# One layer of a hybrid decoder on one core: a written order for the matmuls of the up projection, other buffers for its stored products, and row loads of the down projection tied to the fifth step

## The chip, the core and the metric

The kernel runs on one core of a Trainium2 chip. The metric is device microseconds from the start to the end of one execution; the median of several executions is compared. The core's engines are TensorE (PE, with its weight loads listed as PEld), VectorE (DVE), ScalarE (ACT), GpSimd (POOL) and SyncE (SP). Each works through its own instructions in order; semaphores tie them together. DMA transfers are started here by SP, ACT and POOL.

## The reference

One layer over 1024 positions of width 1024 in float32. The change lies in the last sublayer, a gated feed-forward network with a short causal convolution over positions:

```python
def conv_ffn(h, w_up, dw_w, dw_b, w_down):
    u = causal_dwconv(h @ w_up, dw_w, dw_b)        # FFN_CONV = 3 taps
    gate, val = jnp.split(u, 2, axis=-1)           # 2 x FFN_DIM, FFN_DIM = 2816
    return (jax.nn.silu(gate) * val) @ w_down

    mix = (sigmoid(gate_a) * y_a + sigmoid(gate_b) * y_b) @ w_o[l]
    h = layer_norm(DN_ALPHA * h + mix, ln1_g[l], ln1_b[l])
    h = layer_norm(DN_ALPHA * h + conv_ffn(h, ...), ln2_g[l], ln2_b[l])
```

Before it stand a convolution branch and a state-space branch, which the change doesn't touch.

## The kernel before

**Numbers in two parts.** Every large product is made of float32 operands split into a rounded part and a rest (`split_pair`, L737: ACT casts, DVE subtracts), and `mm3` (L163) issues three matmuls for one product of 128 x 128 by 128 x 512. A product of four contraction tiles (`product`, L725) has 12 matmuls.

**Up projection.** It is done by a scheme with seven products in place of eight: the tokens are cut in halves (early, late), the contraction in halves, and a pair of channel tiles (one gate, one value) makes the 2 x 2 of the weights. `ffn_blocks` (L744) makes the blocks of the activations: b11 and b21 are the two halves of the early tokens, b22 and t1 to t4 are blocks and sums for the late ones. There are NF = 22 pairs. A pair is:

- `up_weights` (L834): two loads (`ra`, `rb`, 512 KB each, in rings `st` and `raw` of three buffers), four additions on DVE, and splits into ue (first weights as they are; from pair 8 on), w24, w10 and w3. ue, w24 and w10 share a ring of three buffers, tag `w` of the pool wsp; w3 has a ring of two.
- `up_rest` (L857): the products. ps is a PSUM bank of the ring `acc` (four), pz one of the ring `sm` (four). b11 goes into ps and is copied to s by ACT; b21 goes into another bank and is added to s for the early tokens of the gate; t2 is added onto ps and copied to s again; t3 goes to pz; t1 onto ps, copied to the value's late tokens; t4 onto pz; b22 onto ps, copied to the gate's late tokens. Then the three taps of the convolution, SiLU and gating (L889 to L916) on ACT and DVE, and the stores of the results, or of sums of two pairs' results, to DRAM (`b11_scr`, `b2_scr`, `t32_scr`, `t41_scr`) from POOL and SP. The gate and the value tile of a pair live in two of three buffers u, in turn, so a pair's gate takes the buffer of the value tile of the pair before.

**The stored products.** For the first LEAD = 8 pairs, `up_first` (L815) computes b11 and b11 + b21 earlier, while the block sums are still being made: two products into one bank, a copy by ACT after each (L831) into a tile `first`, and a store to `first_scr` (L832) from ACT's queue. `first` has a ring of two in a pool of its own, "firsts", on the right side of the memory (L1134). The pair then loads both halves from DRAM into u with one DMA (L874), and ACT copies the late half into ps (L878), where t2 is added onto it.

**The memory.** Pools are stacked from the left or from the right. "trans", the pool of `ffn_blocks`, is on the left and closed before "up" is opened (L1128 to L1130), so both start at the same place; a tile of "up" waits for those tiles of "trans" whose bytes it takes. A pool lays out its tags in the order in which they are first used. In "trans": two gains of 4 KB a partition, three row buffers of 4 KB (tiles r0 to r7; the second buffer is used last by r5, the third by r7), then 16 KB of raw blocks and the temporaries of the sums. In "up": three u of 4224 bytes, then the others.

**Down projection.** `down` (L930) has seven products p = 0 to 6 of eleven steps; a step loads weights and activations (`load`, L974), splits them into w and issues 12 matmuls, three into each of four banks. Its results are combined with the 1024 rows of the residual stream, which `load_rows` (L950) brings from `h1_scr` with four DMAs of 256 KB from POOL, in the code after the fifth step (k = 4) of p = 0, 1, 2 and 4, into one tile `rows`; nothing but the space of that tile holds them back.

**The order.** The program's order on each engine is made by a planner: among the instructions whose inputs it reckons to be there, it takes the one with the lowest number; `tc.high_priority(offset=n)` lowers the number by n. Buffers of a ring are handed out in the order of the code. A block `tc.manual_schedule(engines={PE})` keeps PE's instructions in it in the order of the code.

The products of a pair, before:

```python
ps, pz = bank(1), bank(0)
...
product(ps, lambda i: w24[:, i, :HALF], bl["t2"], False)
A.copy(s, ps)
product(pz, lambda i: w3[:, i], bl["t3"], True)
product(ps, lambda i: w10[:, i, :HALF], bl["t1"], False)
A.copy(uv[:, late], ps)
V.tensor_tensor(out=uv[:, late], in0=pz, in1=uv[:, late], op=ALU.subtract)
product(pz, lambda i: w10[:, i, HALF:], bl["t4"], False)
V.tensor_tensor(out=uv[:, early], in0=pz, in1=s, op=ALU.subtract)
product(ps, lambda i: w24[:, i, HALF:], bl["b22"], False)
A.copy(ug[:, late], ps)
```

Of the kernel before, what the change touches and what calls it, by code (L numbers as in the profile page):

```python
# [16 lines left out]
P = 128  # L17
D = 1024
# [38 lines left out]
def kernel(  # L57
# [17 lines left out]
    def pool(name, bufs=1, **kw):  # L75
        return tc.tile_pool(name=name, bufs=bufs, reuse_waits="tile", **kw)
# [11 lines left out]
    def bank(which):  # L88
        n_ps[0] += 1
        pl, tag = (pacc, "acc") if which else (psm, "sm")  # L90
        return pl.tile([P, 512], F32, tag=tag, name=f"{tag}{n_ps[0]}")
# [633 lines left out]
    def product(ps, w, xs, first):  # L725

        for k in range(4):
            mm3(
                ps,
                lambda i: w(i)[:, k * P : (k + 1) * P],  # L730
                lambda i: xs(i)[:, k, :],
                first and k == 0,
                k == 3,
                not first,
            )
# [76 lines left out]
            "t4": lambda i: b2[0][:, i, 4:8, :],  # L812
        }

    def up_first(upp, fp, bl, j):  # L815

        if j < LEAD - 1:
            t = weights(wup[2 * j], f"ue{j}")
            w = [t[:, i, :] for i in range(2)]
        else:  # L820
            with tc.high_priority(offset=4000):
                st = wst.tile([P, D], F32, tag="st", name=f"st_ue{j}")
                SY.dma_start(st, wup[2 * j])
                w = [upp.tile([P, D], F32R, tag="o", bufs=3, name=f"ue{i}_{j}") for i in range(2)]
                A.copy(w[0], st)
                V.tensor_tensor(out=w[1], in0=st, in1=w[0].bitcast(F32), op=ALU.subtract)
        ps = bank(1)
        for q, block in enumerate(("b11", "b21")):
            product(ps, lambda i: w[i][:, q * HALF : (q + 1) * HALF], bl[block], q == 0)
            f = fp.tile([P, HALF], F32, tag="first", bufs=2, name=f"first{q}_{j}")  # L830
            A.copy(f, ps)  # L831
            A.dma_start(first_scr[j][1 - q], f)  # L832

    def up_weights(upp, j):  # L834


        with tc.high_priority(offset=2000):
            r1 = wst.tile([P, D], F32, tag="st", name=f"ra{j}")
            SY.dma_start(r1, wup[2 * j])
            if j:  # L840
                r2 = upp.tile([P, D], F32, tag="raw", bufs=3, name=f"rb{j}")
            else:
                r2 = wst.tile([P, D], F32, tag="st", name=f"rb{j}")
            SY.dma_start(r2, wup[2 * j + 1])
            a11, a12, a21, a22 = r1[:, :HALF], r1[:, HALF:], r2[:, :HALF], r2[:, HALF:]
            ue = None if j < LEAD else split_pair(wsp, r1, f"ue{j}")
            s3 = upp.tile([P, HALF], F32, tag="s3", name=f"s3_{j}")
            V.tensor_tensor(out=s3, in0=a11, in1=a21, op=ALU.add)
            V.tensor_tensor(out=a21, in0=a21, in1=a22, op=ALU.add)
            V.tensor_tensor(out=a11, in0=a21, in1=a11, op=ALU.add)  # L850
            V.tensor_tensor(out=a12, in0=a12, in1=a11, op=ALU.add)
            w24 = split_pair(wsp, r1, f"s24_{j}")
            w10 = split_pair(wsp, r2, f"s10_{j}")
            w3 = split_pair(upp, s3, f"s3_{j}", HALF, 2)
        return ue, w24, w10, w3

    def up_rest(upp, us, bl, j, before, ws):  # L857

        ue, w24, w10, w3 = ws or up_weights(upp, j)
        ug, uv = us[2 * j % 3], us[(2 * j + 1) % 3]
        s = upp.tile([P, HALF], F32, tag="s", bufs=2, name=f"s{j}")
        early, late = slice(2, 2 + HALF), slice(2 + HALF, 2 + T)
        ps, pz = bank(1), bank(0)
        if ue:
            product(ps, lambda i: ue[:, i, :HALF], bl["b11"], True)
            A.copy(s, ps)
            py = bank(1)
            product(py, lambda i: ue[:, i, HALF:], bl["b21"], True)  # L870
            V.tensor_tensor(out=ug[:, early], in0=s, in1=py, op=ALU.add)
        else:
            with tc.high_priority(offset=2500):
                SY.dma_start(  # L874
                    ug[:, 2 : 2 + T].rearrange("p (q n) -> p q n", q=2),
                    first_scr[j].rearrange("q p n -> p q n"),
                )
            A.copy(ps, ug[:, late])  # L878
        product(ps, lambda i: w24[:, i, :HALF], bl["t2"], False)
        A.copy(s, ps)  # L880
        product(pz, lambda i: w3[:, i], bl["t3"], True)
        product(ps, lambda i: w10[:, i, :HALF], bl["t1"], False)
        A.copy(uv[:, late], ps)
        V.tensor_tensor(out=uv[:, late], in0=pz, in1=uv[:, late], op=ALU.subtract)
        product(pz, lambda i: w10[:, i, HALF:], bl["t4"], False)
        V.tensor_tensor(out=uv[:, early], in0=pz, in1=s, op=ALU.subtract)
        product(ps, lambda i: w24[:, i, HALF:], bl["b22"], False)
        A.copy(ug[:, late], ps)
        os = []  # L889
        j = j // 2 + j % 2 * NK  # L890
        for jj, u in ((j, ug), (NF + j, uv)):
            o = upp.tile([P, T], F32, tag="o", bufs=3, name=f"fo{jj}")
            wc = PC_FW + 3 * jj
            A.activation(  # L894
                out=o, in_=u[:, 2 : 2 + T], func=AF.Identity, scale=pc[:, wc + 2 : wc + 3]
            )
            for k in range(2):
                V.scalar_tensor_tensor(  # L898
                    out=o,
                    in0=u[:, k : k + T],  # L900
                    scalar=pc[:, wc + k : wc + k + 1],
                    in1=o,
                    op0=ALU.mult,
                    op1=ALU.add,
                )
            os.append(o)
        og, ov = os
        A.activation(out=og, in_=og, func=AF.Silu, bias=pc[:, PC_FB + j : PC_FB + j + 1])
        V.scalar_tensor_tensor(
            out=ov,  # L910
            in0=ov,
            scalar=pc[:, PC_FB + NF + j : PC_FB + NF + j + 1],
            in1=og,
            op0=ALU.add,
            op1=ALU.mult,
        )  # L916
        early, late = slice(0, HALF), slice(HALF, T)
        if j < NK:
            G.dma_start(b11_scr[j], ov[:, early])
            return ov  # L920
        SY.dma_start(b2_scr[j - NK], ov)
        a, b, t = before, ov, og
        V.tensor_tensor(out=t[:, early], in0=a[:, late], in1=b[:, late], op=ALU.subtract)
        V.tensor_tensor(out=a[:, late], in0=a[:, early], in1=a[:, late], op=ALU.subtract)
        V.tensor_tensor(out=t[:, late], in0=t[:, early], in1=a[:, early], op=ALU.subtract)
        V.tensor_tensor(out=a[:, early], in0=b[:, early], in1=t[:, late], op=ALU.add)
        G.dma_start(t32_scr[j - NK], t)
        G.dma_start(t41_scr[j - NK], a)

    def down(upp, dp):  # L930
# [16 lines left out]
        E, L = slice(0, HALF), slice(HALF, D)  # L947
        gb = []

        def load_rows(p):  # L950
            t0, cs = {0: (0, E), 1: (0, L), 2: (4, L), 4: (4, E)}[p]
            for t in range(t0, t0 + 4):
                G.dma_start(rs[t][:, cs], h1_scr[t * P : (t + 1) * P, cs])
            if p == 2:
                for n, start in (("g", RW_2G), ("b", RW_2B)):
                    r = upp.tile([P, D], F32, tag="o", bufs=3, name=f"ln2_{n}")
                    G.dma_start(r, prow[start : start + D].partition_broadcast(P))
                    gb.append(r)
# [132 lines left out]
        for p, (banks, first, then) in enumerate(products):  # L1091
            end = NK - LAST if p == 6 else NK
            for k in range(end):
                w = load(p, k)
                for t in range(4):
                    block(banks[t], w, t, first, k)
                if k == 4 and p in (0, 1, 2, 4):
                    load_rows(p)
            ws = {k: load(p, k) for k in range(end, NK)}
            for t in range(4):  # L1100
                for k in ws:
                    block(banks[t], ws[k], t, first, k)
                then(t)
# [27 lines left out]
    us = [upp.tile([P, T + 32], F32, name=f"u{i}") for i in range(3)]  # L1131
    for u in us:
        G.memset(u[:, :2], 0.0)
    with pool("firsts", side="right") as fp:  # L1134
        for j in range(LEAD):
            if j == LEAD - 1:
                ws = up_weights(upp, 0)
            up_first(upp, fp, bl, j)
    before = None
    for j in range(NF):  # L1140
        before, ws = up_rest(upp, us, bl, j, before, ws), None
    ffn_stack.close()
    dp = ctx.enter_context(pool("down", side="right"))
    down(upp, dp)
# [99 lines left out]
```

## Time and profile before

| what | us |
| --- | --- |
| median of 3 executions | 2024.91 (2024.34 to 2026.39) |
| profiled execution | 2030.47 |
| its span, first to last instruction | 2028.8 |
| first matmul of `up_first` in it | 1350.3 |
| last copy of a stored product | 1407.4 |
| first and last row load (L953) issued | 1805.4, 1820.0 |

The profile is of one execution. Its rows give, for each engine, when an instruction started and how long it ran, and in brackets how long the engine had stood idle before and which instruction ended that. Busy time is the time in which an engine ran something; matmuls overlap one another, so their starts say more than their lengths. A row of a window gives its length, then for each engine the busy time and the number of instructions, then the clock that PE was granted (1.00 is full), the busy share of the 16 DMA engines and the GB/s they moved. Some per cent of the matmul records can be missing.

### The profile page before, as it was taken

What the parts mean: (1) busy time and instruction counts of PE and PEld (TensorE: products, weight loads), DVE (VectorE), ACT (ScalarE), POOL (GpSimd) and SP (SyncE); (2) the same over time, 40 slices, a digit from 0 to 9 for tenths busy, and PEclk for the clock granted to TensorE, in tenths of its full rate; (3) what the DMA queues carried; (4) which work ended last, traced back from release to release, by engine and by line L of the source; (5) the groups of instructions that cost most, each with busy time, mean ns of one, the idle gap of its engine ahead of it and who ended that gap; (6) DMA issues with size and microseconds to landing.
All of it is one profiled execution on the core that took longest, in us unless ns stands there. A gap on an engine that the chain in (4) does not pass through costs nothing.

```text
span 2028.8 us, 24542 instructions
## 1 busy us (share of the span) xinstructions
PE 1975.8 (97%) x9164; PEld 1622.4 (80%) x9164; DVE 1695.8 (84%) x2261; ACT 1017.4 (50%) x1480; POOL 175.5 (9%) x140
## 2 busy tenths in 40 slices
PE   7999999999999999999999999999999999999998
PEld 6888888888788888888888888887777777777886
DVE  7599999989766869999998976596897777788768
ACT  4465654556453356665454645364554534443432
POOL 2010101001400000110100130010000000030000
PEclk9999999999999999999999999999999999999999
DMA  6222233333546522222323354565342222367563
GB/s 219 94 64 93 79 103 104 99 104 101 175 131 220 194 94 73 91 81 77 126 89 104 109 167 139 186 234 202 135 172 83 99 107 102 101 252 252 176 225 109
DMA packets 96903, 272.20 MB, mean 134 GB/s; under 512 B 11088, under 2 KB 11088, under 8 KB 96784
## 3 DMA queue, kind: packets, MB, share of 16 engines
q1 hardware_dynamic: 88864, 246.78, 36.8%
q0 software_dynamic: 5616, 19.66, 2.5%
q10 hardware_dynamic: 2304, 4.20, 0.6%
q8 instruction: 72, 1.18, 0.2%
q14 instruction: 47, 0.39, 0.1%
HBM read 221.05 MB, written 49.55 MB: 133 GB/s over the span
## 4 chain that ended last, share of the span: by engine, by line
PE 72%; DVE 19%; DMA 4%; issue 3%; ACT 2%; SPq 0%; DVEq 0%; ACTq 0%
PE acc L166 19%; PE acc L167 19%; PE acc L168 19%; DVE c L420 6%; PE sm L168 3%; PE sm L166 3%; PE sm L167 3%; PE sm L534 2%; PE acc L357 1%; DVE xbc L375 1%; DVE fo L898 1%; DMA dr<-b_scr 1%; PE sm L515 1%; PE sm L192 1%; PE sm L523 1%
## 5 line engine op out<-in xcount | busy, mean ns | idle before, releaser
L420 DVE SCALAR_TENSOR_TENSOR c<-v,pc,c 128x512 f32<-128x512 f32 x480 | 374.9, 804 | 6.3 <-ACT c L409 4.9
L478 POOL TENSOR_TENSOR au<-seg_mv,head_of 128x1024 fp32r<-128x1024 f32 x32 | 76.4, 2388 | 959.1 <-PE sm L487 728.8
L166 PE MATMUL acc<-hT,w_c 128*128 128x512 f32 x352 | 141.0, 401 | 0.0
L167 PE MATMUL acc<-hT,w_c 128*128 128x512 f32 x352 | 140.6, 399 | 0.0
L168 PE MATMUL acc<-hT,w_c 128*128 128x512 f32 x352 | 138.4, 393 | 0.0
L898 DVE SCALAR_TENSOR_TENSOR fo<-u,pc,fo 128x1024 f32<-128x1024 f32 x88 | 111.4, 1279 | 7.5 <-ACT fo L894 7.4
L375 DVE SCALAR_TENSOR_TENSOR xbc<-u,pc,xbc 128x512 f32<-128x512 f32 x144 | 109.9, 775 | 0.7 <-ACT xbc L373 0.5
L166 PE MATMUL acc<-h1s,w_s 128*128 128x512 f32 x264 | 103.6, 396 | 6.3 <-ACT s L880 3.7
L167 PE MATMUL acc<-h1s,w_s 128*128 128x512 f32 x264 | 102.9, 390 | 0.0
L168 PE MATMUL acc<-h1s,w_s 128*128 128x512 f32 x264 | 102.8, 391 | 0.0
L167 PE MATMUL acc<-w_z,hT 128*128 128x512 f32 x256 | 100.8, 394 | 0.0
L166 PE MATMUL acc<-w_z,hT 128*128 128x512 f32 x256 | 100.8, 401 | 0.0
L168 PE MATMUL acc<-w_z,hT 128*128 128x512 f32 x256 | 100.7, 396 | 0.0
L1032 ACT CAST w_dn<-dr 128x1024 fp32r<-128x1024 f32 (+1 forms) x73 | 60.9, 842 | 75.8 <-DVE dr L962 37.8
L154 ACT CAST w_c<-st_c 128x1024 fp32r<-128x1024 f32 x50 | 52.5, 1051 | 88.9 <-PE acc L168 68.2
L1033 DVE TENSOR_TENSOR w_dn<-dr,w_dn 128x1024 fp32r<-128x1024 f32 (+1 forms) x73 | 69.8, 963 | 15.3 <-ACT w_dn L1032 15.1
L167 PEld LDWEIGHTS acc<-hT,w_c 128*128 128x128 f32 x352 | 66.1, 188 | 16.9 <-issue 3.9
L168 PEld LDWEIGHTS acc<-hT,w_c 128*128 128x128 f32 x352 | 66.1, 188 | 16.2 <-issue 2.6
L166 PEld LDWEIGHTS acc<-hT,w_c 128*128 128x128 f32 x352 | 66.1, 188 | 15.9 <-issue 2.6
L166 PE MATMUL acc<-h1b,w_ue 128*128 128x512 f32 x168 | 67.3, 400 | 11.1 <-ACT w_ue L740 8.4
L155 DVE TENSOR_TENSOR w_c<-st_c,w_c 128x1024 fp32r<-128x1024 f32 x47 | 60.5, 1288 | 20.2 <-ACT w_c L154 20.2
L740 ACT CAST w_s<-rb 128x1024 fp32r<-128x1024 f32 x22 | 23.0, 1048 | 98.4 <-PE sm L168 63.8
(353 smaller groups left out, 5755.4 us busy)
## 6 DMA issues: line engine op xcount, KB each, us to landing
st_c<-wcol SPq DMA_DIRECT2D x50, 512.0 KB, 3.5
st_z<-wz SPq DMA_DIRECT2D x32, 512.0 KB, 3.5
st_wo<-wo SPq DMA_DIRECT2D x24, 512.0 KB, 4.0
ra<-wup SPq DMA_DIRECT2D x22, 512.0 KB, 3.6
rb<-wup SPq DMA_DIRECT2D x22, 512.0 KB, 3.4
t_scr<-fo POOLq DMA_DIRECT2D x22, 512.0 KB, 3.8
dr<-t_scr SPq DMA_DIRECT2D x44, 256.0 KB, 3.5
dr<-wdown SPq DMA_DIRECT2D x38, 256.0 KB, 3.9
```

The lines of the kernel that those rows point to most:

```text
L154: A.copy(w[:, 0, :], st)
L155: (eng or V).tensor_tensor(out=w[:, 1, :], in0=st, in1=w[:, 0, :].bitcast(F32), op=ALU.subtract)
L166: TE.matmul(ps, wa(0), xa(0), start=start, stop=False, skip_group_check=more)
L167: TE.matmul(ps, wa(0), xa(1), start=False, stop=False, skip_group_check=more)
L168: TE.matmul(ps, wa(1), xa(0), start=False, stop=stop, skip_group_check=more)
L375: V.scalar_tensor_tensor(out=o, in0=u[:, k : k + HALF], scalar=pc[:, wc + k : wc + k + 1], in1=o, op0=ALU.mult, op1=ALU.add,)
L420: V.scalar_tensor_tensor(out=accs[i], in0=v[:, k : k + HALF], scalar=pc[:, wc + k : wc + k + 1], in1=accs[i], op0=ALU.mult, op1=ALU.add,)
L478: G.tensor_tensor(out=au, in0=seg_mv[:, c, :].unsqueeze(1).to_broadcast([P, 8, P]), in1=head_of[:, g, :].unsqueeze(2).to_broadcast([P, 8, P]),
L534: TE.matmul(py[:, hs], m[:, h, :], xs[:, hs], start=True, stop=True)
L898: V.scalar_tensor_tensor(out=o, in0=u[:, k : k + T], scalar=pc[:, wc + k : wc + k + 1], in1=o, op0=ALU.mult, op1=ALU.add,)
L1032: A.copy(w[:, 0, cs], src)
L1033: V.tensor_tensor(out=w[:, 1, cs], in0=src, in1=w[:, 0, cs].bitcast(F32), op=ALU.subtract)
```

## The change

The stored products take buffers of the ring `s` in the pool "up", which now has three; the pool "firsts" is gone. The order of the two halves in `first_scr` is turned. A pair of the first eight loads the b11 half into its tile s (not into u), copies it into ps from there, and loads the other half into the early tokens of u with a second DMA. The pair's function becomes a generator in three parts, and the caller lays the parts of two pairs over each other: b11 of pair j + 1 (t2 for the first eight); then b22 and t4 of pair j; then b21, t2, t3, t1 of pair j + 1 (t3, t1 for the first eight). b22 now stands before t4. PE keeps that order. Some copies and subtractions get a priority of 300. In the down projection, before the four row loads POOL copies four numbers of the fifth step's w into the first column of the four row blocks, so the loads wait for that w.

```diff
-    def up_first(upp, fp, bl, j):
+    def up_first(upp, bl, j):
-            f = fp.tile([P, HALF], F32, tag="first", bufs=2, name=f"first{q}_{j}")
+            f = upp.tile([P, HALF], F32, tag="s", bufs=3, name=f"first{q}_{j}")
             A.copy(f, ps)
-            A.dma_start(first_scr[j][1 - q], f)
+            A.dma_start(first_scr[j][q], f)
...
-    def up_rest(upp, us, bl, j, before, ws):
+    def up_pair(upp, us, bl, j, kept, ws):
-        s = upp.tile([P, HALF], F32, tag="s", bufs=2, name=f"s{j}")
+        s = upp.tile([P, HALF], F32, tag="s", bufs=3, name=f"s{j}")
+        def t2():
+            product(ps, lambda i: w24[:, i, :HALF], bl["t2"], False)
+            with tc.high_priority(offset=300):
+                A.copy(s, ps)
         if ue:
             product(ps, lambda i: ue[:, i, :HALF], bl["b11"], True)
-            A.copy(s, ps)
+            with tc.high_priority(offset=300):
+                A.copy(s, ps)
+        else:
+            with tc.high_priority(offset=2500):
+                SY.dma_start(s, first_scr[j][0])
+            with tc.high_priority(offset=300):
+                A.copy(ps, s)
+            SY.dma_start(ug[:, early], first_scr[j][1])
+            t2()
+        yield
+        if ue:
             py = bank(1)
             product(py, lambda i: ue[:, i, HALF:], bl["b21"], True)
-            V.tensor_tensor(out=ug[:, early], in0=s, in1=py, op=ALU.add)
-        else:
-            with tc.high_priority(offset=2500):
-                SY.dma_start(
-                    ug[:, 2 : 2 + T].rearrange("p (q n) -> p q n", q=2),
-                    first_scr[j].rearrange("q p n -> p q n"),
-                )
-            A.copy(ps, ug[:, late])
-        product(ps, lambda i: w24[:, i, :HALF], bl["t2"], False)
-        A.copy(s, ps)
+            with tc.high_priority(offset=300):
+                V.tensor_tensor(out=ug[:, early], in0=s, in1=py, op=ALU.add)
+            t2()
         product(pz, lambda i: w3[:, i], bl["t3"], True)
         product(ps, lambda i: w10[:, i, :HALF], bl["t1"], False)
-        A.copy(uv[:, late], ps)
-        V.tensor_tensor(out=uv[:, late], in0=pz, in1=uv[:, late], op=ALU.subtract)
+        with tc.high_priority(offset=300):
+            A.copy(uv[:, late], ps)
+            V.tensor_tensor(out=uv[:, late], in0=pz, in1=uv[:, late], op=ALU.subtract)
+        yield
+        product(ps, lambda i: w24[:, i, HALF:], bl["b22"], False)
+        A.copy(ug[:, late], ps)
         product(pz, lambda i: w10[:, i, HALF:], bl["t4"], False)
         V.tensor_tensor(out=uv[:, early], in0=pz, in1=s, op=ALU.subtract)
-        product(ps, lambda i: w24[:, i, HALF:], bl["b22"], False)
-        A.copy(ug[:, late], ps)
...
-        def load_rows(p):
+        def load_rows(p, w):
             t0, cs = {0: (0, E), 1: (0, L), 2: (4, L), 4: (4, E)}[p]
+            G.tensor_copy(
+                rows.rearrange("p (t n) -> p t n", n=D)[:, t0 : t0 + 4, cs.start : cs.start + 1],
+                w[:, 0, :4].bitcast(F32).unsqueeze(2),
+            )
...
-    with pool("firsts", side="right") as fp:
-        for j in range(LEAD):
-            if j == LEAD - 1:
-                ws = up_weights(upp, 0)
-            up_first(upp, fp, bl, j)
-    before = None
-    for j in range(NF):
-        before, ws = up_rest(upp, us, bl, j, before, ws), None
+    for j in range(LEAD):
+        if j == LEAD - 1:
+            ws = up_weights(upp, 0)
+        up_first(upp, bl, j)
+    kept = []
+    with tc.manual_schedule(engines={mybir.EngineType.PE}):
+        pairs = [up_pair(upp, us, bl, 0, kept, ws)]
+        next(pairs[0])
+        next(pairs[0])
+        for j in range(1, NF + 1):
+            if j < NF:
+                pairs.append(up_pair(upp, us, bl, j, kept, None))
+                next(pairs[j])
+            next(pairs[j - 1], None)
+            if j < NF:
+                next(pairs[j])
```

More of the change, by code (lines that the diff above doesn't have):

```diff
@@ L919, in up_rest @@
             G.dma_start(b11_scr[j], ov[:, early])
-            return ov
+            kept.append(ov)
+            return
         SY.dma_start(b2_scr[j - NK], ov)
-        a, b, t = before, ov, og
+        a, b, t = kept.pop(), ov, og
         V.tensor_tensor(out=t[:, early], in0=a[:, late], in1=b[:, late], op=ALU.subtract)
@@ L1097, in down @@
                 if k == 4 and p in (0, 1, 2, 4):
-                    load_rows(p)
+                    load_rows(p, w)
             ws = {k: load(p, k) for k in range(end, NK)}
```

## The prediction

> **What bounds the kernel now.** I read first the page's busy times and the chain that ended last, then a table of windows over the end of the kernel, then who TensorE (PE) waits for.
>
> ```profile
> span 2028.8 us, 24542 instructions
> PE 1975.8 (97%) x9164; PEld 1622.4 (80%) x9164; DVE 1695.8 (84%) x2261; ACT 1017.4 (50%) x1480; POOL 175.5 (9%) x140
> PE 72%; DVE 19%; DMA 4%; issue 3%; ACT 2%; SPq 0%; DVEq 0%; ACTq 0%
> ```
>
> PE is busy for 97% of the span, and 72% of the chain is PE. The change leaves the number of matmuls as it is, so it can only gain where PE stands still or runs at a low clock, and lose by adding such places. The windows show where these are in the stages that the diff touches.
>
> ```profile
> core 0: us, PE busy (x) PEld busy (x) DVE busy (x) ACT busy (x) POOL busy (x), PEclk, DMA share, GB/s
> 1388.70:1391.50 2.80, 0.07 (x2) 0.04 (x1) 2.27 (x4) 1.17 (x2) 0.00 (x0) 0.85 1.03 417
> 1391.50:1397.40 5.90, 5.90 (x14) 4.64 (x15) 3.44 (x4) 3.45 (x5) 0.00 (x0) 0.50 0.82 303
> 1408.00:1514.00 106.00, 98.65 (x420) 77.51 (x419) 85.85 (x101) 51.84 (x66) 3.95 (x7) 1.00 0.40 139
> 1514.00:1762.00 248.00, 239.59 (x1042) 194.59 (x1041) 193.11 (x222) 112.34 (x137) 10.65 (x20) 1.00 0.29 102
> 1762.00:1796.00 34.00, 33.06 (x143) 26.42 (x142) 28.21 (x29) 16.58 (x20) 6.23 (x7) 1.00 0.47 162
> 1796.00:1806.00 10.00, 9.80 (x43) 7.79 (x42) 8.79 (x10) 6.27 (x9) 2.81 (x4) 1.00 0.26 81
> 1806.00:1824.00 18.00, 17.95 (x79) 14.54 (x79) 14.90 (x18) 9.31 (x13) 8.08 (x15) 1.00 1.02 383
> 1824.00:1836.00 12.00, 8.62 (x27) 6.52 (x26) 7.50 (x13) 4.88 (x9) 1.03 (x2) 0.72 0.81 269
> ```
>
> The yardstick is the step between matmuls of a dense stretch:
>
> ```profile
> 1620.33 0.39 PE L166 MATMUL acc<-h1b,w_ue 128*128 128x512 f32 x1
> 1623.05 0.39 PE L168 MATMUL acc<-h1b,w_ue 128*128 128x512 f32 x1
> ```
>
> Between these two starts lie 12 steps, 2.72 us: 0.227 us a matmul, 2.72 us a product of 12. A window's loss is its length less its count times 0.227.
>
> - First eight pairs (1408 to 1514): 106 - 420 x 0.227 = **10.7 us** lost.
> - Later pairs (1514 to 1762): 248 - 1042 x 0.227 = **11.5 us**.
> - Last pairs (1762 to 1806): 44 - 186 x 0.227 = **1.8 us**.
> - First product of the down stage (1806 to 1836): 30 - 106 x 0.227 = **5.9 us**.
> - Before the pairs: 2.8 us empty, then 14 matmuls in 5.9 us at clock 0.50 where 26 fit, 2.7 us more: **5.5 us**.
>
> Who ended PE's waits from 1200 us on:
>
> ```profile
> PE acc L166 <- ACT w_ue L740: 8.4, 6, 1.4
> PE acc L166 <- ACT s L880: 3.7, 5, 0.9
> PE acc L166 <- ACT w_dn L1032: 3.4, 1, 3.4
> PE acc L166 <- ACT first L831: 2.7, 1, 2.7
> PE acc L166 <- ACT u L883: 2.7, 3, 1.7
> ACT acc L878 <- DMA u<-first_scr: 20.1, 5, 4.5
> ```
>
> A row gives the total in us, the number of waits and the longest. The last row is from 1408 to 1514: the stored product is loaded into u itself, so the load waits until the convolution two tiles earlier has read u, and ACT can fill the bank only then.
>
> **Part by part: later pairs.** Once in 40 us PE reaches the b11 product before its weights are split.
>
> ```profile
> 1637.44 0.39 PE L168 MATMUL acc<-h1s,w_s 128*128 128x512 f32 x1
> 1639.23 0.50 PE L166 MATMUL acc<-h1b,w_ue 128*128 128x512 f32 x1 [1.40 <-ACT w_ue L740]
> 1637.19 1.05 ACT L740 CAST w_s<-rb 128x1024 fp32r<-128x1024 f32 x1 [9.72 <-PE sm L168]
> 1638.14 1.04 ACT L740 CAST w_ue<-ra 128x1024 fp32r<-128x1024 f32 x1
> ```
>
> The step across it is 1.79 us instead of 0.23, with a slow restart of 0.1: 1.67 us, six times, 10.0 of the 11.5. In the written order (b11 of j+1; b22, t4 of j; b21, t2, t3, t1 of j+1) the buffer of ue is free after b21, and t2, t3, t1 (8.2 us) cover the cast and the split. w24 is free after b22 with two products behind it (5.4 us), w10 after t4 with three. Copies of s and u have one product (2.72 us) of cover. What may be late next is the subtraction that frees s: DVE is 78% busy here (193.11 of 248). I take **9 us** gained (bounds 4 and 11.5).
>
> **First eight pairs.** Loading into s removes the chain convolution, DMA, ACT. The load of u's early half still waits for it, but only the next convolution needs that. It becomes two DMAs for one: eight more issues on SP, off the path. DVE is late next: 85.85 us for 420 matmuls is 12.3 us per 60, against 13.6 us of PE, 90%. I take **8 of 10.7** (bounds 0 and 10.7).
>
> **Last pairs.** t1 and b22 of pair 21 follow each other with no pair between, so a copy's wait of about 0.7 us (3.7/5) stays: **1 of 1.8**.
>
> **Down.** All sixteen row loads went out when their tile became free, and share the DMA engines with the loads that PE needs.
>
> ```profile
> 1805.38 3.78 POOL L953 DMA_DIRECT2D rows<-h_scr  x7 [1.70 <-PE sm L168]
> 1819.98 0.55 POOL L953 DMA_DIRECT2D rows<-h_scr  x1 [0.56 <-DMA rows<-h_scr]
> 1812.67 15.16 DMA dr<-b_scr
> dr<-b_scr SPq DMA_DIRECT2D x18, 256.0 KB, 6.9
> L993 POOL COPY c<-dr x5: 614/1517/1646, 1782.0 to 1796.7; 128x512 f32<-128x512 f32 x5
> 1866.00:1896.00 30.00, 30.00 (x134) 24.84 (x133) 28.98 (x42) 12.09 (x16) 0.00 (x0) 1.00 0.60 186
> ```
>
> From 1806 to 1824 the DMA engines are full (share 1.02, 383 GB/s); one load takes 15.16 us instead of the median 6.9, PE waits 3.4 us for its cast, and clock 0.72 follows. With 12 of 16 loads (3 MB, 8 us at 383 GB/s) sent later, that load lands before it is needed. The small copy that ties them is on POOL, busy 9%: four elements a partition, between nothing and the 1.5 us of 512 elements, four times, hidden. It holds a weight buffer until POOL runs; if POOL stands before a store's wait, PE waits too. The rows now fall into products two, three and five, where the DMA share is 0.60 and PE is dense: 0 to 3 us. I take **5 of 5.9** gained (bounds 1 and 5.9).
>
> The Trainium skill, "DMA: Bandwidth & Descriptors", section "Issuing engines are not separate DMA queues", says that transfers issued by different engines share the same 16 DMA engines; the full share at 1806 agrees, and by that rule 3 MB later is work moved, not removed.
>
> **The stored products.** Here I expect a loss. Before, `first` has a pool of its own on the right, free while the block sums are made. After, it takes s buffers of the pool `up`, which lies where the pool `trans` lay. By the tile sizes in the code, u takes 12.4 KB from the common start and the three s buffers 12.4 to 18.4; `trans` has 8 KB of gains, then three row buffers of 4 KB (8 to 20), the second last used by r5, the third by r7. So the first s buffer is free after r5, the two others only after r7 is transposed and stored. That `up` waits for `trans` can be seen: the memsets of u, with no other input, run at 1379.84 on an idle POOL.
>
> ```profile
> 1379.84 0.18 POOL L1133 MEMSET u<- 128x2 f32 x3
> 1370.96 0.33 SPq L779 DMA_DIRECT2D h_scr<-r  x1
> h_scr<-r SPq DMA_DIRECT2D x2, 512.0 KB, 3.4
> L831 ACT COPY first<-acc x16: 573/586/595, 1353.4 to 1407.4; 128x512 f32<-128x512 f32 x16
> DMA to landing us min/median/max: 2.0/3.7/7.0
> 1388.01 0.50 PE L166 MATMUL sm<-h1b,w_s 128*128 128x512 f32 x1
> 1401.73 0.39 PE L166 MATMUL acc<-h1s,w_s 128*128 128x512 f32 x1
> ```
>
> (The fourth row groups the 16 copies of `first`, with first and last start; the landing row is of the transfers through `first_scr`.) r7's store starts at 1370.96 and lands 3.4 us later, 1374.4. Until then PE has four banks and one buffer: five products (b11 of j 0 to 3, b21 of j 0). The second copy ends at 1375.0; eleven products take 29.9 us (1404.9), and after the idle stretch the clock costs 2.7 us as at 1391 (1407.6). Then PE has nothing: s of pair 0 stands sixteen tiles behind `first` in one ring and its buffer comes in the order of the code, t2 of pair 0 is first in the written order, and it needs copy 0.6, load 3.7, copy 0.6: 1412.5, and 2.7 for the clock again: 1415.2. Before, the firsts ended at 1407.2 with t3 and t2 of pair 0 (rows at 1388.01 and 1401.73) done, 5.4 us: as if at 1401.8. The loss is **13 us**, with the 5.5 us of the old gap in it. Bounds: -4 (buffers free as before, and the old gap gone) and 31 (below). Behind the waiting copy on ACT stand casts of block sums and of the next ue, which the order has at their own times, so I charge nothing for them; behind the load of s on SP stand weight loads for pairs 1 and 2, which PE reaches over 13 us later; behind t2 on PE stands everything.
>
> The Trainium skill, "TensorE: Matmul & The Clock Gate", section "HAM oscillation — how this bites in real kernels", says to avoid idle gaps above about 3.4 us. Here a gap of 2.8 us already brought the clock to 0.50. By the page the waits reckoned above, over 4 us each, cost the clock too: the same sum.
>
> **Sum.** -9 - 8 - 1 - 5 + 13 = -10 us, on a profiled execution of 2030.47 us (span 2028.8), which is 0.27% above the median of 2024.91. I take the same 10 us from the median: **2015 us**.
>
> **Rivals.**
> A. The buffers are not held (the planner lets the firsts go on in the one free buffer, or r7 is early). Then only the wait for s of pair 0 stays, 4.9 + 2.7 less the old 5.5: 2 us lost instead of 13, 2004 us. For it: a copy and its store take 0.6 + 4 us, less than two products. Against it: the memsets at 1379.84, and the ring's order.
> B. Slower: all three buffers are held until the last tile of `trans` is read, about 1386 (first cast into `up`, row below). PE then stops after three products (three weight buffers), and thirteen follow: 1386 + 0.6 + 35.4 + 2.7 + 4.9 + 2.7 = 1432, 31 us lost: +8, 2033 us. It decides as soon as the release is 10 us later than 1374.4, after which the 23 us of gains are used up. For it: tiles of `up` start only at 1379 to 1386. Against it: these lie under other tiles than s does.
>
> ```profile
> 1385.88 1.05 ACT L825 CAST ue<-st_ue 128x1024 fp32r<-128x1024 f32 x1
> ```
>
> C. The order does not do what it is written for: DVE, 90% needed in the first eight pairs and in order, becomes the bound, and PE, also in order, cannot go round it. Those pairs keep 106 us per 420 matmuls: 8 us less gain, 2023 us. For it: 85.85 us of DVE. Against it: its waits there are for PE and ACT.
>
> **How the numbers follow.** Forecast 0.48, A 0.19, B 0.15, C 0.18. Low end: A with the upper gains, 2002; high end: near B, 2031. 0.2% (4 us) is about what a measurement of this kernel can tell from no change. Faster by more: 0.43 of the forecast and A, 0.62. Within: 0.05 of the forecast, 0.15 of C, 0.02 of B, 0.22. Slower: 0.13 of B, 0.03 of C, 0.16.
>
> **What the profile after would show.** If I am right: the first copies of L831 come at about 1353, 1374 and 1375; PE is empty for 8 us before 1375 and for 4 to 5 us before the first t2, with low clock behind both; no wait for w_ue in the later pairs; fewer waits in the first eight, at a DVE busy by 90%; row loads in four groups of four, and no wait for w_dn near 1828. A second copy at 1360 would make A right, at 1386 B. A start loss of 5 or 25 us, or pairs at 15 us, would make the forecast wrong.

## The result, and the profile after

The changed kernel takes 2034.92 us (median of 6 executions, 2032.61 to 2038.66); the kernel before, measured beside it, 2026.31 us (6 executions, 2024.34 to 2028.77). The ratio is 1.0044, 95% interval 1.0031 to 1.0056: 9 us slower. The forecast was 10 us faster, and the time lies above the top of the range. The profiled execution of the changed kernel took 2038.66 us.

Its page, the span, the busy times and the chain that ended last:

```profile
span 2036.9 us, 24591 instructions
PE 1975.9 (97%) x9164; PEld 1627.6 (80%) x9164; DVE 1695.1 (83%) x2261; ACT 1022.6 (50%) x1480; POOL 177.7 (9%) x144
PE 74%; DVE 19%; issue 3%; DMA 2%; ACT 1%; SPq 0%; POOL 0%; DVEq 0%; ACTq 0%; POOLq 0%
```

Of this page only the span says that anything went wrong: busy shares are averages over the whole kernel, and 8 us in 2037 are not seen in them. The table of windows says where to look (columns as in the prediction: length; busy time and count of PE, PEld, DVE, ACT, POOL; clock; DMA share; GB/s):

```profile
1362.00:1374.00 12.00, 4.12 (x18) 3.36 (x18) 12.00 (x18) 2.19 (x5) 2.31 (x1) 0.73 0.21 73
1374.00:1386.00 12.00, 2.14 (x10) 1.57 (x8) 10.15 (x16) 5.91 (x12) 2.65 (x5) 0.50 0.16 60
...
1420.00:1520.00 100.00, 91.19 (x384) 73.45 (x383) 77.49 (x93) 50.23 (x65) 3.41 (x6) 0.97 0.44 149
1520.00:1768.00 248.00, 248.00 (x1090) 204.23 (x1089) 206.66 (x237) 125.45 (x146) 11.29 (x21) 1.00 0.31 111
1768.00:1812.00 44.00, 44.00 (x194) 36.22 (x193) 34.01 (x36) 18.88 (x23) 7.40 (x8) 1.00 0.39 131
1812.00:1842.00 30.00, 29.95 (x132) 24.48 (x132) 23.19 (x31) 17.78 (x27) 2.92 (x6) 1.00 0.73 253
```

From 1520 us on PE is dense: 1090 matmuls in 248 us, where there had been 1042, then 194 in 44 us, then 132 in 30 us. What the change was reckoned to bring in the pairs and in the down stage is there. The loss stands between 1362 and 1386 us, where PE is busy for 6 of 24 us. PE's timeline around it (start, length, engine and operation; in brackets the idle time before and what ended it):

```profile
1348.07 1.91 PE L758 MATMUL sm<-ident,r 128*128 128x128 f32 x16
...
1364.97 0.40 PE L168 MATMUL acc<-h1b,w_ue 128*128 128x512 f32 x1
1372.46 3.67 PE L758 MATMUL sm<-ident,r 128*128 128x128 f32 x16 [7.10 <-DVE r L230]
1386.97 0.79 PE L166 MATMUL acc<-h1b,w_ue 128*128 128x512 f32 x1 [10.84 <-ACT first L831]
...
1428.10 0.39 PE L168 MATMUL acc<-h1b,ue 128*128 128x512 f32 x1
1433.80 0.80 PE L166 MATMUL acc<-h1s,w_s 128*128 128x512 f32 x1 [5.32 <-ACT acc L880]
```

PE does three products, stops 7.1 us, makes the last sixteen transposes of the block sums, and stops 10.8 us more, until ACT has made the first copy of a stored product. Then it does the other thirteen and stops 5.3 us for the s of pair 0. Behind each stop the clock is low: the sixteen transposes at 1372 take 3.67 us, where the sixteen at 1348 took 1.91, and two windows behind the other stops stand at 0.50 (the figure after the busy times):

```profile
1386.90:1391.40 4.50, 4.43 (x10) 3.47 (x11) 0.26 (x1) 0.02 (x1) 0.00 (x0) 0.50 0.80 277
1433.80:1439.10 5.30, 5.30 (x13) 4.15 (x14) 0.00 (x0) 1.18 (x2) 0.00 (x0) 0.50 0.19 51
```

Why the first copy comes so late is to be read on ACT's timeline, and the group of L831 gives its first and last start:

```profile
1385.82 0.62 ACT L763 CAST h1b<-ts 128x512 fp32r<-128x512 f32 x1 [2.51 <-DVE ts L794]
1386.34 0.58 ACT L831 COPY first<-acc 128x512 f32<-128x512 f32 x1
```
```profile
L831 ACT COPY first<-acc x16: 577/587/592, 1386.3 to 1428.5; 128x512 f32<-128x512 f32 x16
```

The first copy follows the last cast of `ffn_blocks` (L763) without any idle time of its own: ACT was not waiting for a buffer, the copy simply stood behind that cast in ACT's order, and the cast waited 2.5 us for the last sum. In the kernel before, the first copy ran at 1353.4, ahead of those casts. Nor did the copy wait until all of `trans` was free: VectorE read a tile of it after the copy had begun.

```profile
1386.47 0.69 DVE L764 TENSOR_TENSOR h1b<-ts,h1b 128x512 fp32r<-128x512 f32 x1 [0.68 <-ACT h1b L763]
```

Who ended PE's waits from 1200 us on, the four largest (total us, number, longest):

```profile
PE acc L166 <- ACT first L831: 12.2, 3, 10.8
PE sm L758 <- DVE r L230: 7.1, 1, 7.1
PE acc L166 <- ACT acc L880: 5.3, 1, 5.3
PE acc L166 <- ACT u L893: 2.3, 2, 1.2
```

The waits for w_ue of L740 (8.4 us in six), for s and for w_dn are gone. The first three rows are what is new, all in the start; of the first of them there were 2.7 us before.

**The account.** The changed kernel's profiled execution was late before it reached any code that the change touches. The sixteen transposes of the row at 1348.07 above stand in the timeline of before as

```profile
1343.59 1.91 PE L758 MATMUL sm<-ident,r 128*128 128x128 f32 x16
```

which makes 4.5 us of variation between executions (this one is 3.7 us above its own median). By the reckoning of the prediction the pairs began "as if at" 1401.8 before; here the first t2 starts at 1433.80 and loses 2.7 to the clock, so as if at 1436.5. The start therefore takes (1436.5 - 1348.1) - (1401.8 - 1343.6) = **30.2 us longer**, and the rest, up to the end of the span, (2036.9 - 1436.5) - (2028.8 - 1401.8) = **26.6 us less**. 4.5 + 30.2 - 26.6 = 8.1, the difference of the spans. Without the 4.5 us of variation the two traces lie 3.6 us apart, the medians 8.6: each trace is one execution, so a part of this account is good to some 5 us and no better.

### The profile page after: what moved, and what is told of

It reads as the page before. It is cut to its first block, busy times and chain, and to the rows that moved or that the text cites. A ratio compares the mean times of both kernels' runs of the same rounds, so it can differ in the third digit from the quotient of the medians.

```text
span 2036.9 us, 24591 instructions
## 1 busy us (share of the span) xinstructions
PE 1975.9 (97%) x9164; PEld 1627.6 (80%) x9164; DVE 1695.1 (83%) x2261; ACT 1022.6 (50%) x1480; POOL 177.7 (9%) x144
## 4 chain that ended last, share of the span: by engine, by line
PE 74%; DVE 19%; issue 3%; DMA 2%; ACT 1%; SPq 0%; POOL 0%; DVEq 0%; ACTq 0%; POOLq 0%
PE acc L166 19%; PE acc L168 19%; PE acc L167 19%; DVE c L420 6%; PE sm L166 3%; PE sm L167 3%; PE sm L168 3%; PE sm L534 2%; PE acc L357 1%; DVE xbc L375 1%; PE sm L515 1%; PE sm L192 1%; PE sm L523 1%; DVE w_c L155 1%; DVE x L227 0%
## 5 line engine op out<-in xcount | busy, mean ns | idle before, releaser
L166 PE MATMUL sm<-h1b,w_s 128*128 128x512 f32 x176 | 69.2, 393 | 0.0
```

Source lines behind the costliest of these rows:

```text
L166: TE.matmul(ps, wa(0), xa(0), start=start, stop=False, skip_group_check=more)
```

## The experiments

Two theories stood against each other. **Place:** everything in the pool `up` is set behind the last instruction of the pool `trans` on each engine, since `up` takes its place in the stack. **Bytes:** a buffer of the ring is held only as long as the row buffer of `trans` under it, as the prediction had reckoned. Beside them: what each of the gains is worth by itself, and of what. The runs were measured in two later rounds, in which the kernel before took 2027.87 and 2026.92 us; each ratio is to the one of its own round. Medians of different rounds compare to some 2 us.

### The ring in a pool opened ahead of `trans`

```diff
     qp = ffn_stack.enter_context(pool("ffq", side="right"))
+    ring = ctx.enter_context(pool("ring"))
     with pool("trans") as tp:
...
-            f = upp.tile([P, HALF], F32, tag="s", bufs=3, name=f"first{q}_{j}")
+            f = ring.tile([P, HALF], F32, tag="s", bufs=3, name=f"first{q}_{j}")
...
-        s = upp.tile([P, HALF], F32, tag="s", bufs=3, name=f"s{j}")
+        s = ring.tile([P, HALF], F32, tag="s", bufs=3, name=f"s{j}")
```

> The changed kernel, with its ring s (three buffers, still shared by the stored products and the pairs) in a pool opened before the pool trans, so not where trans lies. Theory 1 (the place of the ring holds the copies of the stored products until the end of the block sums, 30 us; the written order and the later row loads gain 26): the first copy of L831's kind at about 1355 instead of 1386, the second soon after; the wait of 4 to 6 us for s of pair 0 stays, since it stands behind sixteen tiles in the ring; 2004 us (2000 to 2009). Theory 2 (the written order is what costs: PE cannot go round the first t2): no more than 8 us less than after, 2027 to 2035 us.

Measured: 2010.47 us (2008.42 to 2011.06), ratio to before 0.9913 (0.9900 to 0.9927). The copies of L831 and the two stops that are left on PE:

```profile
L831 ACT COPY first<-acc x16: 572/587/591, 1353.5 to 1402.3; 128x512 f32<-128x512 f32 x16
```
```profile
1397.80 0.80 PE L166 MATMUL acc<-h1b,ue 128*128 128x512 f32 x1 [3.49 <-ACT first L831]
...
1404.94 0.80 PE L166 MATMUL acc<-h1s,w_s 128*128 128x512 f32 x1 [2.66 <-ACT acc L880]
```

The first copy is back at 1353.5 and 24 us come back with it, so the hold comes of the place of the ring, not of the ring being shared. The two stops that are left, 3.5 and 2.7 us, each have a restart at half clock behind them (a first matmul of 0.80 us in place of 0.50). The wait for s of pair 0 was expected, and longer; the stop at 1397.8 was not, and the time is 1.5 us over the top of what was expected. The next run shows what both come of.

### A pool of its own for the stored products, as before

```diff
-            f = upp.tile([P, HALF], F32, tag="s", bufs=3, name=f"first{q}_{j}")
+            f = fp.tile([P, HALF], F32, tag="first", bufs=2, name=f"first{q}_{j}")
...
-        s = upp.tile([P, HALF], F32, tag="s", bufs=3, name=f"s{j}")
+        s = upp.tile([P, HALF], F32, tag="s", bufs=2, name=f"s{j}")
...
+    with pool("firsts", side="right") as fp:
```

> The changed kernel, with the pool of before for the stored products (two buffers on the right) and a ring s of two for the pairs. Theory 1: the start is as before, with the short stop of 5.5 us near 1390 and no wait of 4 to 6 us for s of pair 0; all other gains stay; 2001 us (1997 to 2006). If the three buffers of s matter for the pairs: waits for s in the first eight pairs, 2006 to 2012 us. Theory 2: 2027 to 2035 us.

Measured: **2002.31 us** (2001.59 to 2003.1), ratio 0.9875 (0.9861 to 0.9888). It beats both kernels: 1.25% under the one before. All that PE still waits for from 1200 us on, but for 0.2 us:

```profile
PE acc L166 <- ACT acc L880: 2.2, 2, 1.6
PE acc L166 <- ACT first L831: 0.9, 1, 0.9
PE acc L168 <- DVE w_s L741: 0.7, 1, 0.7
PE acc L166 <- ACT u L893: 0.5, 1, 0.5
```

4.5 us in all, and the clock was 1.00 behind the longest. The rest of the change, then, is worth 25 us; the change of the buffers costs 32.6 us by the medians (2034.92 less 2002.31; 34 by the ratios), of which 24.4 are the place behind `trans` and 8.2 the sharing of one ring.

The wait of a copy for a store is not by itself the price of the sharing. ScalarE has it here too, and longer than with the shared ring (3.7 us):

```profile
1398.46 0.59 ACT L831 COPY first<-acc 128x512 f32<-128x512 f32 x1 [4.23 <-DMA first_scr<-first]
```

PE has other work meanwhile: t2 and t3 of pair 0 start at 1395.44 and 1398.18. With one ring, s of pair 0 stands behind sixteen tiles, and t2 started only at 1404.94, behind all the stored products. The stop of 5.5 us with its clock, which was expected to stay near 1390 as in the kernel before, shrank to 0.9 us, so 4 to 5 of the 25 us are this; why it did was not followed up.

### The ring laid behind the last byte of `trans`

```diff
         G.memset(u[:, :2], 0.0)
+    for tag, n, w, bufs in (("s3", 1, HALF, 1), ("w", 2, D, 2), ("o", 3, D, 3), ("raw", 3, D, 3)):
+        for i in range(n):
+            t = upp.tile([P, w], F32, tag=tag, bufs=bufs, name=f"{tag}_place{i}")
+            G.memset(t[:, :2], 0.0)
```

> The changed kernel, with the three s buffers of `up` laid behind the last byte of `trans` (placeholder tiles of the tags s3, w, o and raw are touched first by nine small memsets of POOL; nothing else differs). Theory 1, place in the queue: whatever `up` holds is set behind the last instruction of `trans` on its engine, bytes or no bytes; the first copy of L831 still starts at 1383 to 1387, TensorE still stops about 10 us before it, and the time is that of the changed kernel, 2033 to 2037. Theory 2, bytes of r7 (the step of the prediction): no byte of r5 or r7 is under s any more, the first copies come at about 1354 to 1358, and the time falls by 20 to 26 us to 2009 to 2015.

Measured: 2034.24 us (2033.43 to 2035.65), ratio 1.0034 (1.0021 to 1.0048): no better than the changed kernel. ACT's timeline:

```profile
1383.61 0.62 ACT L763 CAST h1b<-ts 128x512 fp32r<-128x512 f32 x1 [2.51 <-DVE ts L794]
1384.14 0.58 ACT L831 COPY first<-acc 128x512 f32<-128x512 f32 x1
```

With no byte of `trans` under the ring, the copy still stands right behind the last cast. This execution's transposes start 1.8 us earlier than those of the changed kernel (1346.23 and 1348.07), and the copy is 2.2 us earlier. The theory of bytes falls. Whether the program would also wait on a semaphore if the copy stood earlier in the order was not tried.

### The ring in `up` alone, on the kernel before

```diff
-            f = fp.tile([P, HALF], F32, tag="first", bufs=2, name=f"first{q}_{j}")
+            f = upp.tile([P, HALF], F32, tag="s", bufs=3, name=f"first{q}_{j}")
...
-                SY.dma_start(
-                    ug[:, 2 : 2 + T].rearrange("p (q n) -> p q n", q=2),
-                    first_scr[j].rearrange("q p n -> p q n"),
-                )
-            A.copy(ps, ug[:, late])
+                SY.dma_start(s, first_scr[j][0])
+            A.copy(ps, s)
+            SY.dma_start(ug[:, early], first_scr[j][1])
```

> The kernel before, with the stored products in the ring s of `up` and loaded into s, but no written order and the row loads of before: the suspected cost by itself. Theory 1 (the hold is of the ring in `up`, about 30 us, whatever the order): first copy at 1383 to 1387, 25 to 32 us slower in the start, some 4 to 8 us of it given back in the first eight pairs, since the load no longer waits for the convolution: 2046 to 2054. Rival (the hold comes of the written order, which keeps t2 of pair 0 behind all stored products): first copies at 1354, 2018 to 2026.

Measured: 2047.41 us (2044.89 to 2049.8), ratio 1.01 (1.0086 to 1.0114). Its copies:

```profile
L831 ACT COPY first<-acc x16: 577/582/589, 1384.7 to 1435.8; 128x512 f32<-128x512 f32 x16
```

The hold is there without the written order, and it costs 20.5 us net, with whatever the other load gives back; that part was not separated.

### No written order

```diff
-    with tc.manual_schedule(engines={mybir.EngineType.PE}):
+    if True:
```

Once on the changed kernel:

> The changed kernel without the written order (the lines of two pairs still laid over each other in the code, PE's order by the planner). Theory 1: first copy still at 1386; some of the 20 us that the first eight, the later and the last pairs gained goes back: 2040 to 2055 us. Theory 2: PE goes round the waits for s: faster than after, 2010 to 2025 us.

Measured: 2033.35 us (2029.98 to 2036.65), ratio 1.0025 (1.0016 to 1.0034). Neither theory had this. The copies come as late as in the changed kernel (first at 1383.6), but the planner does not stop before t2 of pair 0 as the written order does:

```profile
1436.28 0.50 PE L166 MATMUL acc<-h1s,w_s 128*128 128x512 f32 x1 [1.66 <-ACT acc L880]
```

1.7 us at full clock, in place of 5.3 and 2.7 for the clock. In the pairs two waits for w_ue (1.4 us) and other small ones come back. So with the hold, the written order gives away at the first t2 about what it brings later.

And once on the version with a pool of its own:

> The version with a pool of its own for the stored products (2002.3), without the block that keeps TensorE's order: the worth of the written order with no hold in the way. Theory 1: the waits for w_ue and u in the pairs (10.0 us of 11.5 in the later ones) go because of the written order; without it 6 to 12 us come back: 2008 to 2014. Rival: the order of the code and the loads into s do it, and the planner finds the same order: 2001 to 2004.

Measured: 2011.22 us (2010.48 to 2013.48), ratio 0.9924 (0.9911 to 0.9936), against 0.9875 with the order: the written order is worth 9 us (10 by the ratios) where nothing holds the start, as theory 1 had it. A window over most of the first eight pairs and one over the later ones, with the order:

```profile
1420.00:1500.00 80.00, 77.34 (x337) 62.63 (x336) 74.56 (x87) 45.88 (x57) 3.96 (x7) 1.00 0.48 164
1500.00:1760.00 260.00, 260.00 (x1142) 214.11 (x1141) 214.25 (x247) 128.07 (x151) 11.96 (x23) 1.00 0.30 106
```

and without it:

```profile
1420.00:1500.00 80.00, 75.24 (x312) 60.38 (x311) 66.19 (x76) 40.66 (x51) 3.93 (x7) 0.96 0.44 145
1500.00:1760.00 260.00, 256.52 (x1121) 210.11 (x1120) 213.08 (x244) 123.42 (x149) 11.24 (x21) 1.00 0.31 110
```

Without it 25 matmuls fewer are done in the first window and 21 in the second, at 0.227 us 5.7 and 4.8 us. PE's longest stops without the order:

```profile
1454.84 0.50 PE L168 MATMUL sm<-h1b,w_s 128*128 128x512 f32 x1 [1.89 <-DVE w_s L741]
...
1472.09 0.50 PE L166 MATMUL acc<-h1s,w_s 128*128 128x512 f32 x1 [2.15 <-ACT acc L880]
...
1504.54 0.50 PE L166 MATMUL acc<-h1s,w_s 128*128 128x512 f32 x1 [2.11 <-ACT acc L880]
```

This version is still 15.7 us under the kernel before: the order of the code, with buffers handed out by it, the loads into s, the priorities and the later row loads together bring more than the kept order does.

### The row loads

The kernel before with the tied row loads alone:

```diff
-        def load_rows(p):
+        def load_rows(p, w):
+            G.tensor_copy(
+                rows.rearrange("p (t n) -> p t n", n=D)[:, t0 : t0 + 4, cs.start : cs.start + 1],
+                w[:, 0, :4].bitcast(F32).unsqueeze(2),
+            )
```

> The kernel before, with the tied row loads of the down projection alone. Theory of the prediction: the collision at 1806 to 1836 costs 5.9 us, of which the later loads clear 5; time 2021 to 2023. Rival, from the run of the changed kernel with early loads (one stop of 1.5 us, no low clock): the loads decide little by themselves, and the wait for w_dn at 1828 goes only in part; 2025 to 2027, no difference that can be told. If the tie costs something by itself (POOL's store queue), 2028 or more.

Measured: 2023.34 us (2020.78 to 2026.28), ratio 0.9983 (0.9974 to 0.9992): 3.6 us by the medians, between the two sums. In the trace the collision itself is gone, here at the place of the stop:

```profile
1824.00:1836.00 12.00, 12.00 (x55) 9.94 (x54) 9.69 (x16) 4.95 (x9) 4.53 (x9) 1.00 0.89 279
```

The changed kernel with the row loads of before:

```diff
-        def load_rows(p, w):
+        def load_rows(p):
-            G.tensor_copy(
-                rows.rearrange("p (t n) -> p t n", n=D)[:, t0 : t0 + 4, cs.start : cs.start + 1],
-                w[:, 0, :4].bitcast(F32).unsqueeze(2),
-            )
```

> The changed kernel with the row loads of before (all sixteen as soon as their tile is free). Both theories on the start say nothing of it. If the later row loads are what cleared the first product of the down stage: full DMA engines again, a stop of 3 us with low clock behind it, 6 us more than after, 2041 us. If the written order alone moved the loads apart: 2035 us.

Measured: 2037.31 us (2033.36 to 2038.33), ratio 1.0042 (1.0030 to 1.0055), the same as the changed kernel within the intervals. The collision is there, with full DMA engines, but only one stop comes of it, and no low clock:

```profile
1834.97 0.50 PE L166 MATMUL acc<-w_dn 128*128 128x512 f32 x1 [1.47 <-ACT w_dn L1044]
```
```profile
1824.00:1836.00 12.00, 10.53 (x45) 8.11 (x45) 5.51 (x8) 3.38 (x6) 2.73 (x5) 1.00 1.04 386
```

So the early row loads cost 5.9 us in the trace of one kernel and 1.8 (12 - 45 x 0.227) in that of the other. The slowest load of the activations (`dr`) takes as long in both, 15.2 and 15.5 us, so PE must come upon it later in the second; that the written order leaves it more lead is argued, not shown. The run with the ring in `up` alone, with early row loads and no written order, has the long stop again: PE waits 3.7 us for w_dn.

## Why the prediction was wrong

The step that failed is the one on **the stored products**: "the first s buffer is free after r5, the two others only after r7 is transposed and stored", hence 1374.4 us and a loss of 13. It argued from bytes and durations, and asked when the memory comes free. What decided was the order that was fixed when the program was made: a tile of `up` is used behind the last instruction of `trans` on its engine. The ring laid beyond `trans` shows that the hold does not come of shared bytes, the pool opened ahead of `trans` that it comes of the place. So the sentence under "The memory", that a tile of `up` waits for those tiles of `trans` whose bytes it takes, names only one of the two things that can hold it, and here not the one that did. The first copy came at 1386.3, where the forecast had three by 1375, and the start lost 30.2 us, not 13. The trace of before had this to show, on two engines; POOL's timeline and ACT's:

```profile
1378.62 1.29 POOL L794 TENSOR_TENSOR ts<-h1raw,ts 128x512 f32<-128x512 f32 x1 [4.66 <-DVE h1s L764]
1379.84 0.18 POOL L1133 MEMSET u<- 128x2 f32 x3
```
```profile
1382.70 1.08 ACT L831 COPY first<-acc 128x512 f32<-128x512 f32 x2 [0.45 <-PE acc L168]
...
1385.36 0.62 ACT L763 CAST h1b<-ts 128x512 fp32r<-128x512 f32 x1 [1.58 <-DVE ts L794]
1385.88 1.05 ACT L825 CAST ue<-st_ue 128x1024 fp32r<-128x1024 f32 x1
```

By the prediction's own layout u takes the bytes of the gains and of the first two row buffers, and nothing reads those any more once the store of r6, begun at 1368.64, has landed, at 1372.7 at the latest (the two last stores took 2.8 and 4.1 us). The memsets came 7 us later, right behind the last instruction of `ffn_blocks` on POOL; and the first cast into a tile of `up` on ACT (ue, L825) came right behind the last cast of `ffn_blocks` there, while copies into the pool on the right (`first`) went ahead of it (this cast had its weights late as well, so the row agrees but would not decide by itself). The prediction used the first row as a sign that `up` waits, and did not ask for what; it put B down to 0.15 with the words that those tiles lie under others. Asked which bytes held the memsets, the answer is none, and that would have spoken for B.

**Rival B** is what happened, step by step: three products, a stop until ScalarE has cast the last tile of `trans`, thirteen products, the wait for s of pair 0. B spoke of buffers that are held until that tile is read; what held the copy was its place behind the cast, and the two end at the same instruction. B's size agrees, 31 us against 30.2, but by some luck, since two of its terms erred and made each other good: counted from the common transposes the release came at 1381.9 on the clock of before (1386.3 less 4.5), 4 us earlier than the 1386 it took, while the thirteen products took 41.5 us (1386.97 to 1428.10, where the last matmul starts, and its 0.39) in place of 38.1 with the clock, since PE also waited there for weights and copies (1.1, 0.2 and 1.2 us). The wait for s was 5.3 us, with 4.9 reckoned.

The other terms, each by the prediction's own yardstick of 0.227 us a matmul:

| term | forecast | measured | how |
| --- | --- | --- | --- |
| later pairs | -9 | -10.9 | 248 - 1090 x 0.227 = 0.6 left of 11.5 |
| first eight pairs | -8 | about -8 | two waits for u (2.3 us) and their restarts left of 10.7 |
| last pairs | -1 | -1.8 | 44 - 194 x 0.227 is 0 |
| down | -5 | -5.9 | 30 - 132 x 0.227 is 0 |
| start | +13 | +30.2 | the account above |

The four gains make about 26.6, as the account by spans does, with 23 forecast; they were right in mechanism and a little small. By the medians the gains are smaller: the version with a pool of its own has them all, and 4 to 5 us more at the start, and is 25 us faster. Of the down term the cause was named too simply: 3.6 us by the medians is what the later loads bring alone. The full 5.9 was read off one profiled execution, which stood 5.6 us above the median it was set against (2030.47 and 2024.91), so a stop of that size need not be in the median execution. That is argued, not shown, and the 3.7 us stop in the trace of the ring in `up` alone speaks against it.

Rival A, buffers not held, is what the pool opened ahead of `trans` makes: 2010.5 us, with 2004 reckoned. It lacked the stop of 3.5 us, with its clock, at 1397.8, where a copy waits for a store to land and PE has nothing else to do. Rival C did not come: DVE is busy for 77.49 us for 384 matmuls in the window from 1420, 12.1 per 60, and PE's waits in it, for the last stored product, for s of pair 0 and for u, all end with ScalarE, none with DVE.

On the clock, the prediction charged 2.7 us for each long stop, and the windows at 0.50 after 1386.9 and 1433.8 nearly bear it out: 4.5 - 10 x 0.227 = 2.2 us and 5.3 - 13 x 0.227 = 2.3 us.

## What to carry to other kernels

Before a buffer is moved to another pool, find out what the program's order makes of that pool: where one pool takes the place of another in the stack, its first use on an engine may be set behind the last use of the old one there (seen here on ScalarE and GpSimd), whatever bytes are shared, and an engine that had filled its waiting time with such work will stand idle. The evidence is in the old trace: an instruction with no other input that starts late, right behind the old pool's last instruction on its engine, shows how long the pool is closed there. And a written order and the buffers it runs on are to be tried apart: here the order, the loads and the priorities brought 25 us, the buffers took 33, and the sum looked like a small loss.

## What was not expected of the hardware

The low clock came after shorter stops than the prediction had in its rows (2.8 us). In the version with the planner's order, two stops of 1.89 and 2.15 us in the first eight pairs (rows above) were each followed by matmuls at half clock, and not at once but some 0.8 to 1.0 us after the restart. A window behind the first, at clock 0.66, and PE's timeline behind the second:

```profile
1455.00:1460.00 5.00, 5.00 (x16) 3.91 (x17) 5.00 (x6) 1.85 (x3) 0.00 (x0) 0.66 0.30 105
```

```profile
1472.65 0.39 PE L168 MATMUL acc<-h1s,w_s 128*128 128x512 f32 x1
1472.89 0.52 PE L166 MATMUL acc<-h1s,w_s 128*128 128x512 f32 x1
1473.20 0.63 PE L167 MATMUL acc<-h1s,w_s 128*128 128x512 f32 x1
...
1475.77 0.63 PE L167 MATMUL acc<-h1s,w_s 128*128 128x512 f32 x1
1476.19 0.50 PE L168 MATMUL acc<-h1s,w_s 128*128 128x512 f32 x1
1476.53 0.40 PE L166 MATMUL acc<-h1s,w_s 128*128 128x512 f32 x1
```

Full speed is a start every 0.23 us; from 1473.2 to 1475.8 it is one every 0.43, and by 1476.5 it is full again, 3.4 us or so. A third stop of 2.11 us, at 1504.54, had no such phase behind it (starts 0.23 us apart from the second on), nor had the stop of 1.7 us at 1436.28 in the changed kernel without the written order. In the run with the ring in `up` alone, stops of 1.94 and 2.14 us, before 1459.9 and 1814.1, were paid for: the clock was 0.66 and 0.69 over the 5 us or so behind them. So around 2 us the length of a stop alone does not decide. The Trainium skill, "TensorE: Matmul & The Clock Gate", section "HAM oscillation — how this bites in real kernels", puts the bound at gaps above about 3.4 us. Four stops of 1.89 to 2.15 us here are under it and were paid for all the same, so the measurement decides. In the ten traces, from 1340 to 1900 us, no stop of 1 to 1.80 us had a low clock behind it (the longest stands before 1457.14 in the kernel before with the tied row loads, clock 1.00), and every stop from 1.89 us on had one, but for that of 2.11.
